# A hybrid attention layer on one core: the mixer's heads as slots in a hand-written TensorE order, the indexer's scores by token tile

## The chip, the cores and the metric

The kernel runs on one core of one Trainium2 chip. The metric is the device time of one execution in microseconds (us), as the median of several runs. TensorE (PE) does matmuls and transposes, VectorE (DVE), ScalarE (ACT) and GpSimd (POOL) work on elements, and SyncE (SP) issues most DMAs.

## What is computed

One decoder layer over 512 tokens with a model width of 1024: a half-step gated feed-forward, a mixer of two groups of heads side by side, a second half-step feed-forward. The mixer is the part that matters here.

```
n  = mod2(PreNorm2(h1));  P = n @ W_in      # q, k, v of group A and B, and q_idx (8 x 64), k_idx (64), w_idx (8)
# group A, 8 heads of 64: sparse attention
ki = rmsnorm(k_idx, g_kidx)
score[t,s] = sum_h w_idx[t,h] * relu(q_idx[t,h] . ki[s]),  -inf where s > t
idx = top_k(score, 128)                     # per token, shared by the heads
attnA = softmax(q.k * D**-0.5 + bias[t5_bucket(t - idx)]) @ v     # over idx alone
# group B, 8 heads of 64: stick-breaking, strictly causal
z = q.k * D**-0.5
between = lax.cumsum(u, axis=3, reverse=True) - u     # u = log_sigmoid(-z) where s < t
attnB = exp(log_sigmoid(z) + between) @ v
o  = [RMSNorm_A(attnA) ; RMSNorm_B(attnB)] @ W_out
```

## The kernel before

**Precision.** Matmuls run on a pair: an operand rounded by ACT (`wh`, line 132) and the rest of it, subtracted on DVE or POOL (`wl`, line 138, the method `split`). A product of 512 columns is three matmuls (`mm3`, lines 276 to 278).

**Stages.** The modulation and the first feed-forward fill the span up to about 404 us, the mixer the span from there to about 735 us, the second feed-forward the rest. The change lies in the mixer alone.

**The indexer.** `proj_block` computes the indexer's keys, its weights and three of its four blocks of queries in four PSUM banks, one half of the tokens after the other. When a bank is complete, its end runs: `end_ki` squares the keys on ACT, takes the rstd on POOL, scales the keys into `k2` (line 716, eight DVE instructions), transposes `k2` on PE (line 719), multiplies by the gain (line 721) and splits the result; `end_q` splits a block of queries and three DMAs on the SP queue lay its halves out for the two heads (`stack`, line 784). Then come the scores: for head after head, of each the token tiles 1, 2 and 3 (256, 384 and 512 keys), two matmuls (793 and 794), a relu on ACT (740) and a weighted sum on DVE (741). Each ends with a `fill`, one step of the next unit's projections.

**Top-k.** `topk` finds the 128 highest scores of a token by 16 rounds of MAX8 (line 772) and MATCH_REPLACE (775) on DVE, and at the end marks the others (`ns`, 778). The rounds of the three tiles are interleaved and handed out after the four units of group B; where they come in DVE's queue is up to the scheduler.

**Units.** A unit is two heads: four of group B, then four of group A. Its projections are 12 steps of six matmuls (four for k, four for q, four for v), plus the loads of their weights. Steps are handed out by `fill` while the unit before works. `end_k` and `end_q` split and stack, `end_q` with its low part on POOL; `end_v` copies by ACT (829), transposes on PE (832) and splits. In `unit`, a head's four score tiles go through `attn_b` (mask matmul 900, two sigmoids 902 and 903, scan 904, product 906) or `attn_a` (mask 919, a DVE reduction 921, exponential 923). `transposed` turns the result in three groups (line 888) and splits them into `pt`, then come the product with v (863), ACT's copy `ot` (868), its transposes (871), and the sum of its two halves (874, 875).

**Order.** No order is written by hand: the scheduler sets one static order for each engine from the program's order, the data and the free buffers. Score tiles live in PSUM banks called `at`, of which there are three; transposes go to `tp`.

Of the kernel before, what the change touches and what calls it, by code (L numbers as in the profile page):

```python
# [23 lines left out]
NT = S // 128  # L24
# [40 lines left out]
class Block:  # L65
# [222 lines left out]
    def proj_block(self, ws, n, banks, ends=()):  # L288

        late = self.turned  # L290
        for half in range(2):
            c = slice(half * 256, half * 256 + 256)
            for b, ((w, m), ps) in enumerate(zip(ws, banks)):
                terms = [(w[0], n[0]), (w[0], n[1]), (w[1], n[0])] if half == 0 else \
# [269 lines left out]
    def o_norm(self, grp, o, oT, tp, pool, bufs=4):  # L564
# [14 lines left out]
        for i in range(NT):  # L579
# [5 lines left out]
            self.normed = self.split(oT[0][:, :, ts], oT[1][:, :, ts], x, nc.vector if i % 2 else nc.gpsimd)  # L585

# [4 lines left out]
    def mixer_out(self, oa, oTb, begun):  # L591
        tc, tp = self.tc, self.tp
        with tc.tile_pool(name="mw", bufs=8, reuse_waits="tile") as mw, \
                tc.tile_pool(name="mo", bufs=4, reuse_waits="tile") as pool:
            oT = [[pool.tile([128, 4, S], F32R, tag=f"oT{c}", name="oT", bufs=1) for c in range(2)], oTb]
            self.o_norm(0, oa, oT[0], tp, pool)
# [8 lines left out]
    def mixer(self, n, po, oT):  # L605
# [3 lines left out]
        with tc.tile_pool(name="mu", bufs=1, reuse_waits="tile") as self.upool, \  # L609
# [3 lines left out]
            steps, ready = zip(*[self.qkv_steps(*c) for c in cols])  # L613
            self.steps = steps[0]
            notsel, top, load = self.indexer()
            o = po.tile([128, NT, 512], F32, tag="oab", name="ob")
            with tc.issue_after(load.ins):
                for n_, (_, _, _, u) in enumerate(cols):
                    if n_ + 1 < len(cols):
                        self.steps = steps[n_ + 1]  # L620
                    else:
                        self.steps, banks = self.out_steps(oT)
                    ou = o[:, :, u * 128:(u + 1) * 128]
                    if n_ < 4:
                        self.unit(ready[n_], self.attn_b, ou)
                        continue
                    if n_ == 4:
                        for step in top:
                            step()
                        U = self.bias_windows()  # L630
                        self.o_norm(1, o, oT, tp, pool, 3)
                        o = po.tile([128, NT, 512], F32, tag="oab", name="oa")
                    den = self.small.tile([128, 4, 2], F32, tag="den", name="den", bufs=2)
                    rd = self.small.tile([128, 4, 2], F32, tag="rd", name="rd", bufs=2)
                    ou = o[:, :, u * 128:(u + 1) * 128]
# [5 lines left out]

    def out_steps(self, oT):

        banks = [self.bank(p) for p in (self.pj, self.pj, self.pj, self.at)]
        cks = []

        def load(n):
# [30 lines left out]
    def indexer(self):  # L678
# [74 lines left out]
        for f in todo + scores(6) + scores(7):  # L753
            f()
            self.fill()
# [204 lines left out]
```

## Time and profile before

| what | value |
|---|---|
| median of three runs | 1100.08 us (1098.58 to 1100.43) |
| the profiled execution's own time | 1099.78 us |
| its span in the trace | 1098.0 us |
| PE busy | 1056.6 us, 96% |
| DVE busy | 583.5 us, 53% |
| ACT busy | 405.6 us, 37% |
| POOL busy | 146.0 us, 13% |

The profile is one execution as the hardware profiler saw it. The span is the time from its first instruction to its last. An engine is busy while an instruction runs on it; a wait is the idle time ahead of an instruction, with what ended it. "PEclk" is the TensorE clock that was granted, as a share of full speed.

### The profile page before, as it was taken

The numbers are of one execution on the slowest core, as the hardware profiler recorded it, in microseconds if no ns is written. First come the engines' busy times: TensorE is split into PE (matmuls) and PEld (weight loads), VectorE is DVE, ScalarE is ACT, GpSimd is POOL, SyncE is SP. The second block draws the span as 40 slices with busy tenths as digits, with TensorE's granted clock in tenths as the row PEclk, the third lists the DMA queues.
The fourth block names the chain that finished last, engine by engine and source line by source line (L and its number), as shares of the span: only waits on it lengthen the run. The fifth ranks groups of instructions, "written<-read, shape, count | busy, mean of one in ns | idle before, by whom it ended". The sixth has DMA issues, their size and how long they took to land.

```text
span 1098.0 us, 13367 instructions
## 1 busy us (share of the span) xinstructions
PE 1056.6 (96%) x5111; PEld 869.1 (79%) x5111; DVE 583.5 (53%) x988; ACT 405.6 (37%) x711; POOL 146.0 (13%) x103
## 2 busy tenths in 40 slices
PE   3899999999999998999999999999999999999997
PEld 2778888888888888877777878789888888888886
DVE  5979888834223174499995444582333333322313
ACT  3342222222212363455556656472232222221221
POOL 2000000000000522423332413320000000000030
PEclk9899999999999999999999999999999999999999
DMA  9969887732222503533334433303333333222222
GB/s 282 294 210 325 297 283 266 248 96 95 91 89 92 164 20 93 144 96 96 92 97 142 132 101 110 116 21 114 96 96 96 96 96 96 96 96 96 96 77 77
DMA packets 171364, 146.06 MB, mean 133 GB/s; under 512 B 7132, under 2 KB 142460, under 8 KB 171300
## 3 DMA queue, kind: packets, MB, share of 16 engines
q1 hardware_dynamic: 169792, 142.97, 42.4%
q10 hardware_dynamic: 1508, 2.24, 0.6%
q8 instruction: 40, 0.66, 0.2%
q14 instruction: 24, 0.20, 0.1%
HBM read 132.04 MB, written 2.13 MB: 122 GB/s over the span
## 4 chain that ended last, share of the span: by engine, by line
PE 82%; DVE 8%; issue 3%; DMA 3%; POOL 2%; ACT 1%; SPq 1%; DVEq 0%; POOLq 0%; ACTq 0%
PE mm L276 15%; PE mm L277 15%; PE mm L278 15%; PE mm L319 8%; PE mm L320 8%; PE mm L318 8%; PE mm L298 3%; PE mm L468 2%; DVE at L904 1%; DMA ra<-in_w_ada_dram 1%; PE at L793 1%; PE at L794 1%; PE tp L888 1%; DMA kq<-kq 1%; POOL rstd L143 1%
## 5 line engine op out<-in xcount | busy, mean ns | idle before, releaser
L132 ACT ACTIVATE wh<-raw 128x1024 fp32r<-128x1024 f32 x156 | 164.3, 1058 | 432.0 <-PE mm L277 139.4
L276 PE MATMUL mm<-nl,wh 128*128 128x512 f32 x808 | 321.2, 398 | 0.0
L277 PE MATMUL mm<-nh,wh 128*128 128x512 f32 x808 | 316.3, 392 | 0.0
L278 PE MATMUL mm<-nh,wl 128*128 128x512 f32 x808 | 316.1, 391 | 0.0
L138 DVE TENSOR_TENSOR wl<-raw,wh 128x1024 fp32r<-128x1024 f32 (+1 forms) x120 | 147.0, 1227 | 223.7 <-ACT wh L132 223.5
L278 PEld LDWEIGHTS mm<-nh,wl 128*128 128x128 f32 x808 | 151.8, 188 | 31.4
L276 PEld LDWEIGHTS mm<-nl,wh 128*128 128x128 f32 x808 | 152.3, 188 | 28.8 <-ACT wh L132 0.3
L277 PEld LDWEIGHTS mm<-nh,wh 128*128 128x128 f32 x808 | 152.0, 188 | 29.0
L320 PE MATMUL mm<-wh,hT 128*128 128x512 f32 x352 | 138.9, 394 | 0.0
L319 PE MATMUL mm<-wh,hT 128*128 128x512 f32 x352 | 138.8, 394 | 0.0
L318 PE MATMUL mm<-wl,hT 128*128 128x512 f32 x288 | 113.9, 396 | 0.0
L138 POOL TENSOR_TENSOR wh<-raw,wh 128x1024 fp32r<-128x1024 f32 x10 | 25.2, 2534 | 653.7 <-ACT wh L132 653.6
L521 DVE TENSOR_TENSOR sg<-sg,mm 128x512 f32<-128x512 f32 x44 | 30.1, 685 | 105.1 <-PE mm L278 91.0
L138 POOL TENSOR_TENSOR wl<-raw,wh 128x1024 fp32r<-128x1024 f32 x27 | 64.7, 2397 | 106.3 <-ACT wh L132 98.1
L320 PEld LDWEIGHTS mm<-wh,hT 128*128 128x128 f32 x352 | 66.2, 188 | 15.6
L319 PEld LDWEIGHTS mm<-wh,hT 128*128 128x128 f32 x352 | 66.2, 188 | 15.5
L153 DVE SCALAR_TENSOR_TENSOR acc<-ra,sc,acc 128x1024 f32<-128x1024 f32 x49 | 62.7, 1279 | 4.5 <-DMA ra<-in_w_ada_dram 4.0
L318 PEld LDWEIGHTS mm<-wl,hT 128*128 128x128 f32 x288 | 54.1, 188 | 13.1
L468 PE MATMUL mm<-nh,wh 128*128 128x512 f32 x96 | 33.7, 429 | 7.2 <-ACT nh L447 6.9
L132 ACT ACTIVATE hT<-sg 128x512 fp32r<-128x512 f32 x44 | 27.8, 632 | 27.4 <-DVE sg L521 27.4
L138 DVE TENSOR_TENSOR pt<-tp,pt 128x512 fp32r<-128x512 f32 (+1 forms) x48 | 27.2, 594 | 18.8 <-ACT pt L132 18.7
L793 PE MATMUL at<-kq 128*128 128x256 f32 (+2 forms) x88 | 31.3, 357 | 3.4 <-DMA kq<-kq 3.4
(208 smaller groups left out, 1244.9 us busy)
## 6 DMA issues: line engine op xcount, KB each, us to landing
ra<-in_w_ada_dram SPq DMA_DIRECT2D x56, 512.0 KB, 5.6
raw<-in_w_ffn_gate_dram SPq DMA_DIRECT2D x44, 512.0 KB, 4.2
raw<-in_w_ffn_up_dram SPq DMA_DIRECT2D x44, 512.0 KB, 4.3
raw<-in_w_ffn_down_dram SPq DMA_DIRECT2D x44, 512.0 KB, 3.4
raw<-in_w_in_dram SPq DMA_DIRECT2D x28, 512.0 KB, 3.5
kq<-kq SPq DMA_DIRECT2D x84, 128.0 KB, 2.4
ra<-in_w_ada_dram SPq DMA_DIRECT2D x32, 256.0 KB, 5.5
raw<-in_w_out_dram SPq DMA_DIRECT2D x8, 512.0 KB, 3.8
```

What stands on the lines that cost most here:

```text
L132: return self.nc.scalar.activation(hi, src, AF.Copy)
L138: return a, (eng or self.nc.vector).tensor_sub(lo, src, hi.bitcast(F32))
L153: nc.vector.scalar_tensor_tensor(acc, raw, sc[:, k:k + 1], acc, op0=ALU.mult, op1=ALU.add)
L276: nc.tensor.matmul(ps[0:m, c], w[0][:, k, :], n[1][:, k, c], start=k == 0, stop=False)
L277: nc.tensor.matmul(ps[0:m, c], w[0][:, k, :], n[0][:, k, c], start=False, stop=False)
L278: return nc.tensor.matmul(ps[0:m, c], w[1][:, k, :], n[0][:, k, c], start=False, stop=k == KD - 1)
L298: mm = self.nc.tensor.matmul(ps[0:m, c], wt[:, k, :], nt[:, k, c], start=j + k == 0, stop=j == 2 and k == KD - 1)
L318: nc.tensor.matmul(ps, lh[:, t], wl, start=n == 0, stop=False)
L319: nc.tensor.matmul(ps, ll[:, t], wh, start=False, stop=False)
L320: nc.tensor.matmul(ps, lh[:, t], wh, start=False, stop=n == len(ks) - 1)
L468: nc.tensor.matmul(banks[j], ws[j][l][:, k, :], n[r][:, k, :], start=k + o == 0, stop=k == KD - 1 and o == 2)
L793: nc.tensor.matmul(ps, q[hd][:, t], kl[hd][:, 0:n], start=True, stop=False)
```

## The change

`unit` falls apart into `product`, `output` and `transposed(h, g)`, and a new function `slot` writes one PE order for the whole mixer after the indexer. A slot handles two heads: of the new head the four score tiles, of the one before it the transposes, the product and the output.

```
+    def slot(self, new, old):
+        for i in range(NT):
+            if new:
+                new["tile"][i]()
+            self.fill()
+            if old and i < 3:
+                self.transposed(old, i)
+        if old:
+            self.fill()
+            self.product(old)
+            self.fill()
+            self.output(old)
+        else:
+            self.fill(2)
```

The mixer calls it under `manual_schedule`, which makes PE's order the program's; the other engines keep the order that the scheduler finds.

```
-            with tc.issue_after(load.ins):
+            with tc.issue_after(load.ins), tc.manual_schedule(engines={mybir.EngineType.PE}):
...
+                for u in range(len(cols)):
+                    self.steps = steps[u + 1]
+                    if u == 4:
+                        for f in top:
+                            f()
+                        U = self.bias_windows(scr)
...
+                        if u == 4 and hd == 1:
+                            for k, f in enumerate(self.o_norm(1, self.o, oT, tp, pool, 3)):
+                                self.steps[2 + k] = both(f, self.steps[2 + k])
...
+            gap = [lambda: None]
+            steps.append([outs[0]] + gap * 2 + [outs[1]] + gap * 2 + [outs[2]] + gap * 2 + [outs[3]] + gap * 2 + outs[4:])
```

So the steps of the last unit are the first products with `w_out`, with empty steps between them, and the norm of group B's output (`o_norm(1)`) is spread over four steps of one slot. The indexer's keys are scaled in two DVE instructions, and their transposes become a call of their own (`end_ki2`), which `proj_block` makes just ahead of the second half of its last bank.

```
-            for i in range(NT):
-                for c in range(2):
-                    nc.vector.tensor_scalar(k2[:, i, c, :], kk[:, i, :], r[:, i:i + 1], None, op0=ALU.mult)
+            nc.vector.tensor_mul(k2[:, :, 0, :], kk, r.unsqueeze(2).to_broadcast([128, NT, 64]))
+            nc.vector.tensor_copy(k2[:, :, 1, :], k2[:, :, 0, :])
...
-        todo = [f for hd in range(6) for f in scores(hd)]
+        todo = [score(*c) for c in [(1, hd) for hd in range(6)] + [(2, hd) for hd in range(3)]
+                + [(1, 6), (1, 7)] + [(2, hd) for hd in range(3, 8)] + [(3, hd) for hd in range(8)]]
...
+        for k, f in enumerate(todo):
+            f()
+            self.fill()
+            if k > 6:
+                tops[0].pop(0)()
+                tops[0].pop(0)()
+        return notsel, tops[0] + [f for fs in zip(*tops[1:]) for f in fs], load
```

The scores go by token tile, tile 1 first and tile 3 last, and 26 of the 33 top-k operations of tile 1 are handed out among the last 13 scores. Two subtractions of the indexer's weights move from POOL to DVE, and the rows of the bias are made earlier (`bias_rows`).

On PE around the indexer's keys (`k` is `k2`, `at` is the fourth bank), before:

```order
L298 MATMUL mm<-nh,wl 128x256 x8
L298 MATMUL mm<-nl,wh 128x256 x8
L298 MATMUL mm<-nh,wh 128x256 x3
L719 MATMUL tp<-ident,k_3174 128x128
L298 MATMUL mm<-nh,wh 128x256 x2
L719 MATMUL tp<-ident,k_3174 128x128
L298 MATMUL mm<-nh,wh 128x256 x2
L719 MATMUL tp<-ident,k_3174 128x128
L298 MATMUL mm<-nh,wh 128x256
L719 MATMUL tp<-ident,k_3174 128x128
L298 MATMUL mm<-nh,wl 128x256 x8
```

and now (line 300 was 298, line 744 was 719, lines 823 and 824 were 793 and 794):

```order
L300 MATMUL mm<-nh,wh 128x256 x8
L300 MATMUL mm<-nh,wl 128x256 x8
L300 MATMUL mm<-nl,wh 128x256 x8
L744 MATMUL tp<-ident,k_3174 128x128 x4
L300 MATMUL at<-nh,wh_3033 128x256 x8
L300 MATMUL at<-nh,wh_3034 128x256 x8
L300 MATMUL at<-nl,wh_3033 128x256 x8
L276 MATMUL mm<-nl,wh 128x512
L277 MATMUL mm<-nh,wh 128x512
L278 MATMUL mm<-nh,wl 128x512
```

The four transposes of the keys stand 21 matmuls later, in one piece.

The first unit's steps run out at the thirteenth of the twenty scores that are handed out after the fourth block of queries, so the last seven, all of 512 keys, stand on PE without a step of a projection between them.

On PE at the end of a unit's projections in group A (line 862 was 832, line 921 was 871), before:

```order
L919 LDWEIGHTS negi
L919 MATMUL at<-ns,negi 128x256
L276 MATMUL mm<-nl,wh 128x512
L832 MATMUL tp<-ident,vt 128x128 x4
L871 MATMUL tp<-ident,ot 128x128 x4
```

and now:

```order
L276 MATMUL mm<-nl,wh 128x512
L277 MATMUL mm<-nh,wh 128x512
L278 MATMUL mm<-nh,wl 128x512
L862 MATMUL tp<-ident,vt 128x128 x4
L921 MATMUL tp<-ident,ot 128x128 x4
L823 MATMUL at<-kq 128x256
```

The transposes of v now stand right behind the last matmul of v, and nothing lies between them but ACT's copy.

On DVE, the last instructions of the top-k (772, 775, and 778 with `ns`) and the work around them, before:

```order
L772 MAX m_4808<-tk 128x8
L775 MATCH_REPLACE tk<-m_4804,tk 128x256
L775 MATCH_REPLACE tk<-m_4806,tk 128x384
L138 TENSOR_TENSOR pt<-tp,pt 128x512 x2
L775 MATCH_REPLACE tk<-m_4808,tk 128x512
L138 TENSOR_TENSOR pt<-tp,pt 128x256
L778 TENSOR_TENSOR ns<-tk,sco 128x256
L778 TENSOR_TENSOR ns<-tk,sco 128x384
L778 TENSOR_TENSOR ns<-tk,sco 128x512
L875 TENSOR_TENSOR ob<-ob,tp 128x4x64
```

and now, around the scan (958) and the product behind it (960) of the sixth head of group B:

```order
L805 MATCH_REPLACE tk<-m_4786,tk 128x512
L958 SCALAR_TENSOR_TENSOR at<-at,ones 128x384
L138 TENSOR_TENSOR pt<-tp,pt 128x256
L960 TENSOR_TENSOR x<-at,x 128x383
L958 SCALAR_TENSOR_TENSOR at<-at,ones 128x512
L808 TENSOR_TENSOR ns<-tk,sco 128x384
L960 TENSOR_TENSOR x<-at,x 128x511
L808 TENSOR_TENSOR ns<-tk,sco 128x512
L138 TENSOR_TENSOR v<-tp,v 128x8x64
L925 TENSOR_TENSOR ob<-ob,tp 128x4x64
```

Before, the three `ns` stood behind the last scan and product of the eighth head; now the top-k ends with those of the sixth, and tile 1's `ns` stands in the first head's slot.

## Rows read from the trace of the kernel before

**Rows 1.** The page: the span, and busy time by engine.
```profile
span 1098.0 us, 13367 instructions
PE 1056.6 (96%) x5111; PEld 869.1 (79%) x5111; DVE 583.5 (53%) x988; ACT 405.6 (37%) x711; POOL 146.0 (13%) x103
```

**Rows 2.** Waits of PE in the mixer: who waited for whom, total, times, longest.
```profile
PE at L793 <- DMA kq<-kq: 3.4, 4, 1.2
PE tp L719 <- DVE k L716: 2.9, 2, 1.9
PE tp L888 <- DVE x L906: 2.3, 5, 0.6
```

**Rows 3.** Busy time in one stretch: length, PE, PEld, DVE, ACT, POOL, PEclk, DMA.
```profile
480.00:500.00 20.00, 18.52 (x101) 14.72 (x99) 19.77 (x51) 9.24 (x20) 7.09 (x4) 1.00 0.40 111
```

**Rows 4.** All engines around one unit's q and the next scores.
```profile
516.01 0.59 ACT L823 ACTIVATE q<-mm 128x512 f32<-128x512 f32 x1
518.19 1.46 PE L863 MATMUL at<-pt,v 128*128 128x512 f32 x8
519.49 0.44 PE L276 MATMUL mm<-nl,wh 128*128 128x512 f32 x1
522.07 0.39 PE L278 MATMUL mm<-nh,wl 128*128 128x512 f32 x1
523.20 0.35 PE L793 MATMUL at<-kq 128*128 128x256 f32 x1 [0.73 <-DMA kq<-kq]
```

**Rows 5.** The granted clock (the number after POOL) behind the second wait for the keys.
```profile
430.00:432.00 2.00, 2.00 (x12) 2.00 (x11) 1.30 (x3) 1.11 (x2) 0.00 (x0) 0.52 0.83 242
```

**Rows 6.** PE's instructions around the indexer's keys: start, length, what, idle before.
```profile
428.82 0.33 PE L719 MATMUL tp<-ident,k 128*128 128x128 f32 x1 [1.90 <-DVE k L716]
429.55 1.61 PE L298 MATMUL mm<-nh,wl 128*128 128x256 f32 x8
434.91 1.07 PE L298 MATMUL at<-nl,wh 128*128 128x256 f32 x8
```

**Rows 7.** Line 716, the eight scalings of the keys: shortest, median, longest in ns.
```profile
L716 DVE TENSOR_SCALAR k<-kk,rstd x8: 242/243/2387, 425.9 to 429.2; 128x64 f32<-128x64 f32 x8
```

**Rows 8.** POOL's instructions at the same time.
```profile
426.20 2.35 POOL L138 TENSOR_TENSOR wl<-raw,wh 128x1024 fp32r<-128x1024 f32 x1 [0.36 <-ACT wh L132]
```

**Rows 9.** The SP queue behind the keys: the DMAs of the pairs.
```profile
431.76 6.63 SPq L784 DMA_DIRECT2D kq<-kq  x8
```

**Rows 10.** The page: the pairs' DMAs: count, KB each, median us from issue to landing.
```profile
kq<-kq SPq DMA_DIRECT2D x84, 128.0 KB, 2.4
```

**Rows 11.** DVE in the mixer by shape: the weighted sum of 512 keys.
```profile
L741 DVE SCALAR_TENSOR_TENSOR sco<-at,wix,sco 128x512 f32<-128x512 f32 x7 | 5.2, 747 | 4.5 <-ACT at L740 4.4
```

**Rows 12.** DVE at the end of the top-k: start, length, what.
```profile
569.63 0.41 DVE L775 MATCH_REPLACE8 tk<-m,tk 128x256 f32<-128x256 f32 x1
569.96 0.08 DVE L775 MATCH_VALUE_LOAD tk<-m,tk 128x8 f32 x1
```

**Rows 13.** DVE from 440 to 580 us by line: busy, mean ns, idle before.
```profile
L904 DVE TENSOR_TENSOR_SCAN at<-at,ones 128x128 f32<-128x128 f32 (+3 forms) x32 | 25.7, 817 | 0.2
L775 DVE MATCH_REPLACE8 tk<-m,tk 128x256 f32<-128x256 f32 (+2 forms) x45 | 24.1, 542 | 0.0
L772 DVE MAX8 m<-tk 128x8 f32<-128x256 f32 (+2 forms) x45 | 23.3, 546 | 0.0
L906 DVE TENSOR_TENSOR x<-at,x 128x127 f32<-128x127 f32 (+3 forms) x32 | 14.8, 476 | 0.0
L138 DVE TENSOR_TENSOR pt<-tp,pt 128x512 fp32r<-128x512 f32 (+1 forms) x24 | 13.5, 590 | 0.2
L778 DVE TENSOR_TENSOR ns<-tk,sco 128x256 bf16<-128x256 f32 (+2 forms) x3 | 4.3, 1478 | 0.0
```

**Rows 14.** All engines around one unit's v: start, length, what, idle before.
```profile
493.53 0.39 PE L278 MATMUL mm<-nh,wl 128*128 128x512 f32 x1
493.95 0.60 ACT L829 ACTIVATE vt<-mm 128x512 f32<-128x512 f32 x1 [3.63 <-PE mm L278]
```

More of the change, by code (lines that the diff above doesn't have):

```diff
@@ L286, in proj, with proj_block @@
         return ps
[L288 removed]
+    def proj_block(self, ws, n, banks, ends=(), mids={}):
         late = self.turned
@@ L585, in o_norm @@
             self.normed = self.split(oT[0][:, :, ts], oT[1][:, :, ts], x, nc.vector if i % 2 else nc.gpsimd)
+        return [lambda i=i: one(i) for i in range(NT)]
     def bank(self, pool):
@@ L612, in mixer @@
             cols = [(C_QB, C_KB, C_VB, u) for u in range(4)] + [(C_QA, C_KA, C_VA, u) for u in range(4)]
-            steps, ready = zip(*[self.qkv_steps(*c) for c in cols])
-            self.steps = steps[0]
-            notsel, top, load = self.indexer()
-            o = po.tile([128, NT, 512], F32, tag="oab", name="ob")
-            with tc.issue_after(load.ins):
[L618 to L635, printed above, removed]
-                    self.unit(ready[n_], lambda hd, qk: self.attn_a(hd, qk, U[u * 2 + hd], notsel, den), ou)
-                    nc.vector.reciprocal(rd, den)
-                    ou = ou.rearrange("p i (h n) -> p i h n", h=2)
-                    nc.vector.tensor_mul(ou, ou, rd.unsqueeze(3).to_broadcast([128, 4, 2, 64]))
@@ L640, in mixer @@
-        return o, banks
+            first, steps, ready = map(list, zip(*[self.qkv_steps(*c) for c in cols]))
+            both = lambda *fs: lambda: [f() for f in fs]
+            loads, outs, banks = self.out_steps(oT)
+            for u in range(len(cols) - 1):
+                steps[u][8] = both(first[u + 1], steps[u][8])
+            for k, f in zip((4, 8), loads):
+                steps[-1][k] = both(f, steps[-1][k])
+            gap = [lambda: None]
+            steps.append([outs[0]] + gap * 2 + [outs[1]] + gap * 2 + [outs[2]] + gap * 2 + [outs[3]] + gap * 2 + outs[4:])
@@ L642, in out_steps @@
+        return self.o, banks
     def out_steps(self, oT):
-        banks = [self.bank(p) for p in (self.pj, self.pj, self.pj, self.at)]
-        cks = []
+        banks, cks = [], []
         def load(n):
@@ L892, in attn_b, with product @@
-    def attn_b(self, hd, qk):
+    def slot(self, new, old):
[10 more added lines that the diff above has]
+            self.output(old)
+        else:
+            self.fill(2)
+    def product(self, h):
+        nc, pool, at = self.nc, self.pool, self.at
+        v, hd = h["v"]["v"], h["hd"]
+        ps = at.tile([128, 512], F32, tag="at", name="at")
+        c = 0
+        for j in range(NT):
+            w = (NT - j) * 128
+            for p in h["pt"]:
+                nc.tensor.matmul(ps[:, j * 128:512], v[:, j, hd, :], p[:, PT_OFF[j]:PT_OFF[j] + w],
+                                 start=c == 0, stop=c == 7)
+                c += 1
+        h["ot"] = pool.tile([128, 512], F32, tag="w2", name="ot", bufs=3)
+        nc.scalar.activation(h["ot"], ps, AF.Copy)
```

142 lines of the change are left out of this document (79 added, 63 removed).

## The prediction

> **What bounds the kernel now.** I read the page first: PE is busy 1056.6 of 1098.0 us [rows 1]. The reader is to see that only some 41 us of the span have no matmul, and that the change, which adds and removes no matmul, can win only from PE's waits and from time at the lower clock. The order of the two programs outside the mixer is the same, so I read the waits of PE in the mixer alone [rows 2]. Three kinds matter: four waits for the DMAs that stack q or k (3.4 us), two for the indexer's scaled keys (2.9), five of a head's transposes for DVE's product (2.3). The last kind comes from a stage in which DVE is full: 19.77 of 20 us while PE has 18.52 [rows 3], and its scans, products and top-k instructions there wait for hardly anything [rows 13]. In that stage it is DVE's work, and where it stands, that sets what PE can do.
>
> **What the change takes away.** A wait costs more than its idle time: the matmul before it lasts 0.39 us, and without a wait the next would start 0.23 us after its start (eleven starts in 2.58 us, from 519.49 to 522.07) [rows 4]. So I add 0.16 us to each.
>
> The waits for DMA: from ACT's copy of q to the first scores with it 7.2 us pass, with PE waiting 0.73 at the end [rows 4]. In the new order the last matmul of q is the second step of a slot. Behind it come four steps of six matmuls (1.39 us each by the pitch of 0.23), a product of 1.3 (518.19 to 519.49 [rows 4]), five groups of transposes (some 1.4) and two score tiles (some 1.1): 9.4 us. That is over the 7.2 by more than the longest of these waits, 1.2 [rows 2]. All four go: 3.4 + 4 x 0.16 = 4.0 us.
>
> The five waits of transposes for DVE go as such, 2.3 + 5 x 0.16 = 3.1 us, and what DVE asks for instead is counted below.
>
> The keys: the two waits are 2.9 us and 0.3 for their ends. Behind them PE ran at 0.52 of its clock, the lower of its two levels (1.2 of 2.4 GHz), for much of 430 to 432 us [rows 5], after an idle of 1.90 [rows 6] and shortly before the other 1.0 of the 2.9 [rows 2]. The 32 matmuls from 429.55 to 434.91 took 5.36 us, where eight at the full clock take 1.07 less 0.16, so 32 take 3.6 [rows 6]; the clock cost 1.7. In all 4.9 us are lost here. What stays: the new transposes stand 21 matmuls later, at about 427.6 us by a pitch of 0.115. Of the eight scalings one took 2.387 us and the median 0.243 [rows 7]; the long one lies over a POOL subtraction from 426.20 to 428.55 [rows 8], and the second wait ended just behind that. The new form has two instructions on DVE from 425.9 on, of about 0.4 each (256 elements took 0.41 [rows 12]), so the second again meets POOL's start at 426.2. If it is blocked, the keys are ready at 428.9, and PE waits 1.3 us. Then the scores: from the last transpose to the DMAs of the pair [rows 9], which start 431.76 in the trace, some 2.4 us pass, and the landing takes 2.4 as the median of the pairs' DMAs [rows 10]; the new order has 24 + 6 matmuls there, 4.2 us, so 0.7 more is waited. I take both, 2.3 with their ends, and a full clock: the gain is 4.9 - 2.3 = 2.6 us, with 4.4 at the upper end and 1.0 at the lower (with the lower clock again).
>
> The Trainium skill, SBUF — State Buffer, "Who interferes with whom", says that a DVE instruction in a mode with two ports, such as a copy or a scaling of 32-bit data, and a GpSimd instruction hold the shared ports in turn, and that the later one is blocked for the whole of the other. It speaks against this edit: the number of DVE instructions is cut, but not the wait behind POOL. Rows 7 agree. By it the sum stands at 2.6; if the new pair slipped past, at 4.4.
>
> Together: 4.0 + 3.1 + 2.6 = 9.7 us.
>
> **What the change costs.** *The end of the indexer.* The last seven score tiles, of 512 keys each, stand together. On PE one is two matmuls of 0.23, 0.46. On DVE it is a sum of 0.747 [rows 11], of which some 0.08 overlaps with the next (a 0.41 long instruction whose follower starts 0.33 on [rows 12]), and between them DVE's order has one of tile 1's top-k instructions, some 0.35: 1.03 a tile. The relu adds some 0.6 ahead of the first (512 columns took ACT 0.60 [rows 14]), and v's low part 0.6 of DVE. PE has three banks, so the fifth of the eleven tiles from there needs the bank of the second, and so on; the first head's first tile comes at about 6.3 us from the start of the seven, where PE's own work is 3.6. I take 2.7 us, between 1 (if DVE's top-k work slipped behind) and 5 (with the lower clock).
>
> *The heads of group B.* DVE's work in the first six slots, from rows 13 with 0.08 off for each instruction: scan and product of a head (25.7 + 14.8 - 5.1) / 8 = 4.4, six heads 26.5. Top-k: 24.1 + 23.3 less 7.2 is 40.2 for 15 rounds of three tiles, with the first round and the value loads 46.3, of which tile 1 has about a quarter, and 26 of its 32 operations are done before: 37.2 remain. The marks 4.3. The low parts of `pt` 1.45 a head, five heads 7.2. Low parts of v and k and the sums of the outputs, 5. Together 80 us. PE's work in the same slots: six steps 8.3, score tiles 1.8, transposes 1.1, product 1.3, output 0.4, and v's transposes 0.4 in every second: 13.3 or 12.9, and 10.4 in the first: 76 us. Before, the same work had eight heads' time; now, by the order, the last mark stands in the sixth slot, and slots seven and eight leave DVE half empty. So PE waits for 4 us at least. Going along the order by hand, it waits in four places for together 10 (the second, third and fifth slot's transposes, and v's transposes of the sixth, since ACT's queue holds a DMA for a buffer of the top-k ahead of v's copy). I take 7 us, nearer to the sum, range 3 to 11.
>
> *Transposes of v.* In every slot that ends a unit's projections they stand right behind v's last matmul. ACT's copy starts 0.42 us after that matmul's start and lasts 0.60 [rows 14], so PE goes on at 1.03 where it could at 0.23: 0.8 us. In the first units DVE's wait covers it; in the four last it is paid, 3.2 us.
>
> *Rest.* The norm of group B's output stands in one slot with its chain ACT, DVE, POOL ahead of its transposes: 0.5, between 0 and 2. In the last unit the step ahead of `output` is empty, so that `ot` waits for its copy as v does, in two slots: 1.6.
>
> Together: 2.7 + 7.0 + 3.2 + 0.5 + 1.6 = 15.0 us. Against 9.7 that is 5.3 slower: the profiled execution would go from 1099.8 to 1105.1 us. It stands 0.3 below the median of 1100.08, so the forecast is 1105.4.
>
> **The rivals.** *DVE keeps up (faster).* If the heads' work on DVE trails by less than PE's banks and buffers allow, the first two costs fall to 1 and 1, the keys slip past POOL (4.4) and the rest stays: 11.5 - 7.3 = 4.2 faster, 1095.9; with half of v's waits covered too, 1094. For it speaks that PE in the present order waits only 2.3 us for a DVE that is just as full [rows 2, 3]; against it that the same work now has six slots. It decides where PE's waits in the six slots sum to under 2 us. *The gains and costs cancel.* With 3 for the heads and 1 for the indexer's end, costs and gains are 9.3 and 9.7: 1099.7. *The clock drops (slower still).* If the indexer's end or two of the slots idle as the keys do now, each drop costs what it did there, 1.7 [rows 6, 5], and the heads cost 10: 1105.4 + 3 + 3.4 = 1112. The wait is then one of two or more of over 1 us close together; a lone idle of 0.88 in 480 to 500 left that stretch at 1.00 [rows 3].
>
> The Trainium skill, TensorE: Matmul & The Clock Gate, "HAM oscillation — how this bites in real kernels", says that short bursts of matmuls between waits are throttled again and again. By that rule every slot with two waits would pay as the keys did, six slots 10 us, 1115; rows 5 bear it out at one place only, and rows 3 speak against it for single waits. I give it 3 in 100.
>
> **How the numbers follow.** The forecast with its near bounds (over 1102.3) has 0.40, the drop of the clock in one or two places 0.09, in every slot 0.03: slower by over 0.2% (about what a measurement of this kernel can tell from no change) 0.52. Cancelling has 0.14. DVE keeping up has 0.34. The range from 1093 to 1111 leaves out the throttled slots and the far ends, about 1 or 2 in 10; cases of both signs hold most of the chance, and the forecast's own range is 1102 to 1110.
>
> **What would show it.** Right: no wait for DMA on the stacked pairs in group B; a wait of about 1 us at line 744 behind POOL; waits at lines 823 and 942 between the indexer's end and the sixth slot that sum to near 10; waits of 0.8 at line 862 in group A. DVE full from the indexer's end to the sixth slot and half empty behind it. Wrong, if PE's busy share in the six slots stays as it is: then DVE trails without harm, and the time falls. Wrong too if line 744 has no wait, or if the granted clock is below 1.00 in the heads.

## The result, and the profile after

The changed kernel takes 1115.24 us (median, 1113.62 to 1117.01) where the one before took 1099.89 beside it: 1.0142 times as long, with a 95% interval from 1.0124 to 1.0160. The forecast was 1105.4, in a range up to 1111. The sign came as forecast, the size was a third of what came, and the time lies above the range. The profiled execution took 1115.25 us with a span of 1113.4, so 15.4 us were added to the 1098.0 of [rows 1].

The waits of PE in the mixer, changed kernel (who waited for whom: total, times, longest), stand against [rows 2]:

```profile
PE tp L862 <- ACT vt L859: 7.4, 7, 1.6
PE at L823 <- DMA kq<-kq: 4.6, 2, 2.7
PE tp L202 <- DVE pt L138: 3.3, 2, 2.0
PE at L823 <- DVE sco L767: 2.1, 4, 1.1
...
PE tp L921 <- ACT ot L911: 1.5, 2, 0.7
...
PE tp L942 <- DVE pt L138: 0.8, 3, 0.3
PE tp L942 <- DVE v L138: 0.6, 1, 0.6
```

The reader is to see that of the three kinds of [rows 2] two are gone (the keys, line 719 before and 744 now, and the heads' products, 888 and 942), and that five others have come (a sixth, of 0.2 us, is not listed). All waits of the mixer sum to 23.6 us in 28 places, where the kernel before had 12.2 in 19. With 0.16 us for the end of the matmul ahead of each, as in the prediction, that is 12.8 us more.

The rest is the clock. The stretches behind two of the waits (length, PE, PEld, DVE, ACT, POOL, PEclk, DMA), changed kernel:

```profile
470.00:472.00 2.00, 2.00 (x8) 1.61 (x7) 1.18 (x5) 0.10 (x1) 0.00 (x0) 0.51 0.22 59
472.00:474.00 2.00, 2.00 (x7) 1.52 (x7) 1.41 (x5) 0.56 (x2) 0.00 (x0) 0.63 0.00 0
610.00:612.00 2.00, 2.00 (x6) 1.58 (x5) 1.11 (x2) 0.84 (x2) 0.74 (x1) 0.50 0.03 8
612.00:614.00 2.00, 2.00 (x11) 1.80 (x11) 0.00 (x0) 0.01 (x1) 0.54 (x1) 0.65 0.00 0
```

PE ran at the lower of its levels for much of the next 4 us each time, as it had behind the keys in [rows 5]: two drops where there was one. PE was busy all through these stretches, so what the clock lacks to 1.00 in each, times its 2 us, is time lost: 0.98 + 0.74 = 1.7 us behind the first wait and 1.7 behind the second, the price of the prediction. One drop more and 12.8 us of waits are together 14.5 of the 15.4 us.

The shares by term, each with 0.16 for every wait, forecast and measured in the two profiles (two kinds of 0.3 and 0.2 us, one gone and one new, are left out):

| term | forecast | measured |
|---|---|---|
| the keys, with their lower clock | -2.6 | -4.9 |
| waits for the pairs' DMAs | -4.0 | +0.9 |
| the heads' transposes for DVE | -3.1 + 7.0 | -2.3 |
| the indexer's end, DVE's sums | +2.7 | +2.7 |
| transposes of v | +3.2 | +8.5 |
| the norm of group B | +0.5 | +3.6 |
| the last unit's outputs | +1.6 | +1.8 |
| splits of `pt` in group A | 0 | +0.9 |
| the clock, behind the indexer's end and the norm | 0 | +3.4 |
| sum | +5.3 | +14.6 |

Where the largest new waits come from can be read in the same trace. **The pairs.** The SP queue's DMAs of the second unit's q, and the score that waits for them:

```profile
489.89 8.98 SPq L814 DMA_DIRECT2D kq<-kq  x3
```
```profile
498.40 0.46 SPq L814 DMA_DIRECT2D kq<-kq  x1
```
```profile
kq<-kq SPq DMA_DIRECT2D x1, 128.0 KB, 8.4
```
```profile
499.06 0.36 PE L823 MATMUL at<-kq 128*128 128x256 f32 x1 [2.71 <-DMA kq<-kq]
```

The first line spans the issues of all three and not a landing; the second is the issue of the third DMA alone. That DMA overwrites what the first one reads, and is issued only at 498.40. The third line, from the list of DMA issues (count, size, us from issue to landing), shows why: the first DMA, issued at 489.89, landed 8.4 us later, where [rows 10] has 2.4 as the median of one and where the same DMA of the kernel before took 3.9. At 489.14 to 491.3 four loads of the bias windows (256 KB each) were issued from ACT's queue. The other wait of the 4.6, 1.90 us at 468.80, is the first unit's; ACT's rows show why:

```profile
453.79 0.58 ACT L853 ACTIVATE q<-mm 128x512 f32<-128x512 f32 x1
...
460.03 0.61 ACT L859 ACTIVATE vt<-mm 128x512 f32<-128x512 f32 x1 [0.81 <-PE mm L278]
460.54 0.64 ACT L132 ACTIVATE kq<-q 128x512 fp32r<-128x512 f32 x1
```

The copy of q was ready at 454.4, and its rounding came at 460.5, where the kernel before had 0.3 us between them. The rounding waits for a buffer: there are 13 of the kind `kq`, and scores by token tile keep the four blocks of indexer queries alive until the tiles of 512 keys. That is read from the program; the run with scores in pairs tests it.

**v.** Four of the seven waits are for ACT's copy alone (0.69 to 0.75 us). In the other three ACT had something else ahead; here a rounding of weights, in ACT's order ahead of the copy:

```profile
643.11 1.06 ACT L132 ACTIVATE wh<-raw 128x1024 fp32r<-128x1024 f32 x1 [0.66 <-PE mm L277]
644.08 0.58 ACT L859 ACTIVATE vt<-mm 128x512 f32<-128x512 f32 x1
```
```profile
644.71 0.66 PE L862 MATMUL tp<-ident,vt 128*128 128x128 f32 x4 [1.46 <-ACT vt L859]
```

**The norm.** DVE's scalings of line 584, POOL's rows beside them, and the transposes behind:

```profile
602.07 1.29 DVE L584 TENSOR_SCALAR ob<-ob,rstd 128x512 f32<-128x512 f32 x1
...
604.48 3.52 DVE L584 TENSOR_SCALAR ob<-ob,rstd 128x512 f32<-128x512 f32 x2
```
```profile
603.92 2.38 POOL L138 TENSOR_TENSOR wl<-raw,wh 128x1024 fp32r<-128x1024 f32 x1 [0.84 <-ACT wh L132]
606.26 1.45 POOL L138 TENSOR_TENSOR oT<-no,oT 128x512 fp32r<-128x512 f32 x1
```
```profile
609.09 0.63 PE L202 MATMUL tp<-ident,ob 128*128 128x128 f32 x4 [2.04 <-DVE pt L138]
```

The two scalings that fell beside POOL's subtractions took 3.52 us; the first of the four took 0.48. In DVE's order the reduction of a score tile and the split of `pt` stand behind them, so PE waits for the split, though the scalings are what is late.

### The profile page after: what moved, and what is told of

Its sections match the earlier page's. It is cut to its first block, busy times and chain, and to the rows that moved or that the text cites. A ratio compares the mean times of both kernels' runs of the same rounds, so it can differ in the third digit from the quotient of the medians.

```text
span 1113.4 us, 13353 instructions
## 1 busy us (share of the span) xinstructions
PE 1061.4 (95%) x5104; PEld 871.0 (78%) x5111; DVE 588.1 (53%) x984; ACT 408.9 (37%) x711; POOL 141.9 (13%) x101
## 5 line engine op out<-in xcount | busy, mean ns | idle before, releaser
L138 DVE TENSOR_TENSOR wl<-raw,wh 128x1024 fp32r<-128x1024 f32 (+1 forms) x122 | 149.5, 1227 | 241.4 <-ACT wh L132 241.2
L138 POOL TENSOR_TENSOR wl<-raw,wh 128x1024 fp32r<-128x1024 f32 x25 | 60.2, 2410 | 105.1 <-ACT wh L132 98.5
L823 PE MATMUL at<-kq 128*128 128x256 f32 (+2 forms) x88 | 34.6, 394 | 6.8 <-DMA kq<-kq 4.6
```

What stands on the lines that cost most here:

```text
L138: return a, (eng or self.nc.vector).tensor_sub(lo, src, hi.bitcast(F32))
L823: nc.tensor.matmul(ps, q[hd][:, t], kl[hd][:, 0:n], start=True, stop=False)
```

## The experiments

Two theories stood against each other. **Queues (Q):** PE's fixed order meets single late steps, and what is late stands in ACT's, POOL's or the DMAs' queues. **DVE (D):** the prediction's own main cost, DVE's load in the first six slots. The ratios below are to the kernel before, in runs on the same chip; the changed kernel's own is 1.0142.

The clock differs between these runs too, and it has to be kept apart from the waits. In the profiles of scores by head and of later bias windows PE ran at the full clock all through the mixer, so 3.4 us of their gain on the changed kernel's profile are clock; in those of the norm on ACT and of half of the top-k it ran at the lower level for longer than in the changed kernel's. The sections say what that hides.

### The keys' part alone

```diff
-                    nc.vector.tensor_scalar(k2[:, i, c, :], kk[:, i, :], r[:, i:i + 1], None, op0=ALU.mult)
+            nc.vector.tensor_mul(k2[:, :, 0, :], kk, r.unsqueeze(2).to_broadcast([128, NT, 64]))
+            nc.vector.tensor_copy(k2[:, :, 1, :], k2[:, :, 0, :])
...
+                        {3: end_ki2})
```

> The kernel before with the keys' part of the change alone: two DVE instructions for the scaling, and the four transposes 21 matmuls later. In the trace of the change the wait for the keys and the lower clock behind it are gone. If that is due to this part, the time is 4 to 5 us under the kernel before (about 1095.4). If the second DVE instruction is blocked by POOL as the prediction had it, and the change's trace shows no wait only because other work was late there, the gain is 2.6 or less and a wait of about 1 us stands at the transposes.

Measured: 1096.72 us, 0.9952 (0.9935 to 0.9968), so 5.3 us less. In its waits the keys don't stand any more, and the others are those of before, somewhat longer for the DMAs:

```profile
PE at L799 <- DMA kq<-kq: 3.8, 4, 1.3
PE tp L894 <- DVE x L912: 2.3, 5, 0.6
```

This part wins more than the 4.4 us that the prediction had as its upper end, and it is the fastest kernel of the study. Not all of the 5.3 is the keys: the waits and the drop that went are 4.9 us in the profile, and the mean granted clock of the five runs is 0.997 against 0.994 of the kernel before beside them, by estimate some 3 us, where the drop at the keys is 1.7.

### Scores by head again

```diff
-        todo = [score(*c) for c in [(1, hd) for hd in range(6)] + [(2, hd) for hd in range(3)]
...
+        todo = [score(i, hd) for hd in range(8) for i in range(1, NT)]
...
-                tops[0].pop(0)()
```

> The changed kernel with the indexer's scores by head again and no top-k operation among them; slots, keys and all else stay. Theory Q (PE's fixed order is held up at single places, by what stands in ACT's, POOL's and the DMAs' queues): the waits at the indexer's end, 2.1 us for DVE's sums and 1.9 for the pair of the first q, go with the clock's drop behind them, 6 us in all: about 1109. Theory D (DVE has the work of eight heads in six slots): with the 26 early top-k operations moved into the slots, DVE has some 9 us more to do there and PE waits longer: 1115 or more.

Measured: 1108.40 us, 1.0066 (1.0041 to 1.0091), 0.75% less than the changed kernel. Of the waits at the indexer's end 0.8 us are left, and the pair's wait is 0.5. Waits for DVE at v's low part grew from 0.6 to 2.3, which is D's direction, but not its size:

```profile
PE tp L938 <- DVE v L138: 2.3, 2, 1.2
...
PE at L819 <- DVE sco L767: 0.8, 2, 0.6
PE at L819 <- DMA kq<-kq: 0.5, 1, 0.5
```

Of the 8.3 us, 3.4 are the two drops of the clock, which this profile doesn't have. The one behind the norm is gone although the norm's waits, 1.30 and 2.04 us, are those of the changed kernel.

### Scores in pairs of heads

```diff
+        todo = [score(*c) for c in [(1, hd) for hd in range(6)] + [(2, 0), (2, 1), (3, 0), (3, 1)]
+                + [(1, 6), (1, 7)] + [(i, hd) for h in (2, 4, 6) for i in (2, 3) for hd in (h, h + 1)]]
...
```

> The changed kernel with the scores of the tiles 2 and 3 taken in pairs of heads, so that a block of indexer queries is done with early and its buffers come free; tile 1 stays first and its top-k early. Theory Q with buffers as the cause: the rounding of the first unit's q, which stood behind the fourth score tile of 512 keys on ACT, comes some 5 us earlier, the wait of 1.9 us for its pair goes and the seven tiles in a row are broken up: 4 to 6 us less, 1109 to 1111. If the wait is due to the place of q's rounding behind v's copy for another reason, it stays: 1115.

Measured: 1115.33 us, 1.0124 (1.0101 to 1.0147). The mechanism is as expected; ACT's rows:

```profile
455.52 0.58 ACT L853 ACTIVATE q<-mm 128x512 f32<-128x512 f32 x1
...
456.41 0.62 ACT L132 ACTIVATE kq<-q 128x512 fp32r<-128x512 f32 x1
```

The rounding comes with the copy and the first unit's wait for its pair is gone, so the buffers were the cause of this wait. The gain is not there: the second unit's pair then waited 2.94 us, DVE's split of v 3.2 us in two places, and behind both the stretches of 6 us from 494 and from 556 us ran at a granted clock of 0.72. What was saved ahead was waited for later.

### v's transposes later

```diff
+            st["vt"] = vt
+
+        def end_v2():
+            vt = st["vt"]
...
+                steps[u + 1][0] = both(steps[u + 1][0], ready[u]["end_v2"])
```

> The changed kernel with the transposes of v behind the first step of the next slot instead of right behind v's last matmul. Theory Q: seven waits of 0.7 to 1.6 us, 7.4 in all, with 0.16 each for the matmul's end go: 8.5 us less, about 1107. Theory D: the waits at the transposes of v only take up time that PE would wait for DVE anyway in the first units; then three go to waits for DVE, and the gain is 4 to 5: 1110.

Measured: 1110.07 us, 1.0074 (1.0052 to 1.0095), 0.67% less. Six of the seven waits are gone, one of 0.2 is left; the pair of the second unit waited longer:

```profile
PE at L825 <- DMA kq<-kq: 4.3, 1, 4.3
...
PE tp L949 <- DVE ob L932: 2.1, 2, 1.5
```

The waits for v had covered part of the wait for the pair, and part of DVE's.

### The bias windows later

```diff
...
+            self.tc.add_manual_dep(ld.ins, self.ots[-2].ins.name, NOSYNC, reason="issue order")
```

> The changed kernel with all eight loads of the bias windows issued from ACT's queue behind the output copy of the seventh slot, where four of them stood in the second slot and four in the sixth ahead of v's copy. If these loads (1 MB in the second slot) delay the pairs' DMAs, the wait of 2.7 us for the second unit's pair goes, and the wait of 1.6 at the sixth slot's transposes of v falls to 0.7: 3.7 to 4.5 us less, 1111. If DVE's work in the six slots is the bound, this time comes back as waits for DVE: 1114 or 1115.

Measured: 1112.30 us, 1.0090 (1.0074 to 1.0107), 0.51% less. The SP queue's row for the second unit's q:

```profile
489.51 4.30 SPq L816 DMA_DIRECT2D kq<-kq  x3
```

The row is 4.30 us instead of 8.98 (the first DMA lands after 3.8 instead of 8.4), and there is no wait for it; v's wait of 1.6 in the sixth slot is 0.69. At DVE 0.7 us more is waited. So the early loads were the cause of this wait, and DVE took back little. The waits alone explain about half of the 5.7 us; this profile, the fastest of its four, has none of the changed kernel's two drops of the clock.

### The norm's scalings on ACT, and later in the slot

```diff
-            nc.vector.tensor_scalar(o[:, i, :], o[:, i, :], r[:, i:i + 1], None, op0=ALU.mult)
+            nc.scalar.activation(o[:, i, :], o[:, i, :], AF.Copy, scale=r[:, i:i + 1])
```

> The changed kernel with the four scalings of group B's norm on ACT instead of DVE. In the trace of the change they took 0.48, 1.29 and together 3.52 us on DVE, the long ones while POOL made a low part, and PE waited 1.28 and 2.04 us behind them, with the clock at 0.50 and 0.65 of full speed afterwards. If POOL's hold on DVE is the cause: the second wait and the lower clock go, 3.5 to 4 us less, 1111.5; the first stays, since the norm's chain is not done. If the chain itself is too late for its slot: both waits stay, 1115.

Measured: 1117.38 us, 1.0142 (1.0124 to 1.0160): no gain. The two waits of 3.3 us became one of 2.4, for the chain itself:

```profile
PE tp L202 <- ACT ob L584: 2.4, 1, 2.4
```

All waits of the mixer, with their ends, are 1.8 us less than in the changed kernel. The clock hides it: from 460 us on, stretches of 20 us were granted 0.83, 1.00 and 0.91 where the changed kernel had 0.91, 1.00 and 1.00, and 0.91 from 600 on in both. The mean of the four runs is 0.990, that of the changed kernel's four 0.9925.

Then the same with the first three of the four groups one step later:

```diff
-                                self.steps[2 + k] = both(f, self.steps[2 + k])
+                                self.steps[(3, 4, 5, 5)[k]] = both(f, self.steps[(3, 4, 5, 5)[k]])
```

> The changed kernel with the norm's scalings on ACT and its four groups of transposes one to two steps later in the slot (the steps 3, 4, 5, 5 instead of 2, 3, 4, 5). With the scalings on ACT alone one wait of 2.4 us was left, at step 2, for a chain of squares, POOL's rstd and the scaling that is not done by then. If the place in the slot is the rest of the cause, that wait goes and the time falls by the 3.3 us of the two waits and by the lower clock where it follows them: 3.5 to 5 us, 1110 to 1112. If the chain delays something else in the slot (the exponentials of the new head stand behind the scalings on ACT), the gain is under 2.

Measured: 1116.84 us, 1.0144 (1.0122 to 1.0166): again no gain. Of the norm's waits 0.6 us are left, but ACT's queue, which now has the scalings too, made the next transposes of v wait 2.35 instead of 0.75:

```profile
618.23 0.66 PE L862 MATMUL tp<-ident,vt 128*128 128x128 f32 x4 [2.35 <-ACT vt L859]
```

All waits together are 2.5 us less than in the changed kernel, and the time still didn't fall. The profiled execution, the slowest of its four, was granted 0.74 from 460 to 480 us and 0.83 from 500 to 520, against 0.91 and 1.00 in the changed kernel; the mean of the four runs is 0.989. By itself this run settles nothing on the size of the norm's part.

### Half of the top-k

```diff
-            if k > 6:
+            if 6 < k < 15:
...
-        return [top, drop] * (TOPK // 8)
+        return [top, drop] * (TOPK // 16)
...
```

> The changed kernel with half of the top-k: 8 rounds a tile instead of 16, so that the attention of group A sees the 64 highest scores less than it should. It leaves some 20 us of DVE's work out of the first six slots and 1 to 2 out of the indexer's end. Theory D (DVE's load there sets the time): the waits of PE for v, the pair and the sums between 460 and 560 us shrink by 5 or more: 1108 to 1110. Theory Q: of these waits, 2.1 us at the score tiles fall to 1 or so, the pairs' and v's stay as they are: 1113.5 to 1115.

Measured: 1115.95 us, 1.0128 (1.0109 to 1.0147), so 0.14% less, inside the interval of no difference. The stretches of its heads, with DVE's busy time as the third of the busy times, against the 20.00 that DVE was busy from 520 to 540 us in the changed kernel:

```profile
500.00:520.00 20.00, 18.60 (x89) 15.28 (x90) 12.22 (x26) 8.13 (x19) 2.72 (x2) 0.83 0.45 122
520.00:540.00 20.00, 19.31 (x105) 15.41 (x104) 12.35 (x21) 11.81 (x27) 7.09 (x4) 1.00 0.38 106
```

DVE is busy for 12 of 20 us, and PE waits as long for v and the pairs as in the changed kernel: 6.5 + 5.3 us against 7.4 + 4.6. So these waits don't come from DVE's load, and D falls as their explanation. The 0.14% is not the price of that load, though. All waits with their ends are 2.5 us less here, and the profiled execution, the slowest of its four at 1118.61, lost some 4.7 us more to the clock than the changed kernel's, by the same sum as above over stretches of 1 us and PE's busy time in them (it was granted 0.74 from 460 to 480 us and 0.83 from 500 to 520); the mean of the four runs is 0.990. Why the clock was lower no run shows. Under "What DVE's load is worth" the same halving is held against a kernel without a drop on either side.

### Together

The changed kernel with scores in pairs of heads, v's transposes and the bias windows later, the norm's scalings on ACT without their new place, the whole top-k, and besides:

```diff
-            self.fill()
+            if k == 0 or k > 7:
+                self.fill()
...
+                for _ in range(min(3, len(self.top)) if new["u"] < 4 else 0):
+                    t = self.top.pop(0)()
+                    if t is not None:
+                        self.tc.add_manual_dep(t.ins, self.last.ins.name, NOSYNC, reason="issue order")
```

> The changed kernel with all of it together: scores in pairs of heads with the steps of the projections moved to the last of them, the transposes of v behind the next slot's first step, the bias windows behind the seventh slot, the norm's scalings on ACT, and what is left of the top-k handed out three operations behind each score tile of group B, kept there in DVE's order. If DVE had too much in the first six slots, the even hand-out takes that away, and nothing but the norm's first wait, the last unit's two and the tail's is left: 1100 - 5 for the keys - 4 for the pairs - 3 for DVE's products, and 2 to 3 back: 1090 to 1092. If the manual order costs in itself, it stays over the 1095.4 of the keys alone.

Measured: 1106.22 us, 1.0037 (1.0022 to 1.0052). It missed the expected 1090 to 1092 by 14 us. It made waits of its own, 2.8 us of the bias rows' matmul for a bank that DVE's split of k held, and 2.4 for two pairs, and it kept the norm's 2.4:

```profile
PE mm L684 <- DVE kq L138: 2.8, 1, 2.8
PE tp L202 <- ACT ob L584: 2.4, 1, 2.4
PE at L827 <- DMA kq<-kq: 2.4, 2, 1.3
```

So the parts were joined again one by one, on scores by head. First scores by head and v later:

> The changed kernel with two parts mended: the indexer's scores by head, and the transposes of v behind the next slot's first step. Alone the first gave 0.8% and the second 0.7%, and the second was partly given back at the second unit's pair, which waited 4.3 us behind the early loads of the bias windows; by head these loads come after the top-k. Theory Q: the two add up, and no such wait comes: 1.5% to 1.7% under the changed kernel, which is 0.1% under to 0.2% over the kernel before. Theory D: waits for DVE in the heads take their place, and the gain is 1% or less.

Measured: 1102.83 us, 1.0016 (1.0006 to 1.0025): 1.24% less than the changed kernel, where the two alone gave 0.75% and 0.67%. They nearly add up, and no wait for a pair is left. This profile, and those of the next three runs, have no drop of the clock in the mixer, so they can be held against each other by their waits. What DVE takes back is now seen:

```profile
PE tp L202 <- DVE pt L138: 3.3, 2, 2.0
PE tp L945 <- DVE ob L928: 3.0, 3, 1.6
```

With the norm on ACT and later:

> As the kernel with two parts mended, and the norm on ACT and later as well. If the norm's slot gives 3.5 to 5 us by itself, this is 0.2% to 0.5% faster than the kernel before, which is about what the keys' part gives alone: then the slots cost and win nothing once their local waits are gone.

Measured: 1099.17 us, 0.9984 (0.9971 to 0.9997). The norm's part gives 0.32%, 3.5 us, here, where v's transposes don't stand behind ACT's queue: its waits fall from 3.3 to 0.6 and 0.4. With the last unit's products moved:

```diff
-            steps.append([outs[0]] + gap * 2 + [outs[1]] + gap * 2 + [outs[2]] + gap * 2 + [outs[3]] + gap * 2 + outs[4:])
+            steps.append([outs[0]] + gap * 4 + [outs[1], outs[2]] + gap * 4 + [outs[3]] + outs[4:])
```

> As the one with three parts mended, and in the last unit the products with the output's weights stand right ahead of the head's output instead of ahead of its second score tile, so that the copy of the output is covered: two waits of 0.75 and their ends, 1.8 us, go; against it the three groups of transposes there have less between them, and two waits of 0.26 for their splits may grow to 0.6 each. So 0 to 1.8 us under the kernel with three parts: 0.3% to 0.6% faster than before.

Measured: 1098.86 us, 0.9979 (0.9969 to 0.9988). The waits at the outputs fell from 1.5 to 0.4 us, the one at the norm of group A grew by 0.4, and the time by no more than the interval allows. The version that beats both kernels most is still the unit order with the keys' part, 0.9952.

### What DVE's load is worth

> The slots with three parts mended (scores by head, v's transposes later, the norm on ACT and later) and half of the top-k, 8 rounds a tile instead of 16, so that group A's attention sees the 64 highest scores less. In the mended slots 5.4 us of waits for DVE were left before the eighth head, at the score sums, the products, v's low part and the output's sums. If they are DVE's load, 3 to 4 us go: 0.4% to 0.5% under the mended slots, to about 0.994 of the kernel before. If they are chains of single steps, the time stays within 1 us.

Measured: 1098.33 us, 0.9971 (0.9959 to 0.9983), 0.13% less than with the whole top-k, where 0.4% to 0.5% were expected for a load of DVE and under 1 us for chains of single steps: it lies between, at 1.4 us, and far from the 7 us of the prediction. The waits for DVE at the transposes fell from 3.8 us to 1.6, and the ones for ACT's copies (`ot`, and the split of `pt`) grew from 1.7 to 3.0:

```profile
PE tp L945 <- DVE v L138: 0.7, 2, 0.4
...
PE tp L945 <- DVE ob L928: 0.6, 1, 0.6
```

> The kernel before with the keys' part, and half of the top-k in the same way. Its waits for DVE at the transposes are 2.8 us, and the ones for the pairs' DMAs 3.8. If DVE's load is behind the first only: 2.5 to 3 us less than with the keys alone, 0.993. If PE's order, which the scheduler writes anew, moves the DMAs' waits too, more. The two kernels with half of the top-k are then to be held against each other: equal means that the slots' order costs nothing beyond DVE; the slots over 1 us slower means that something else of theirs stays.

Measured: 1098.77 us, 0.9978 (0.9969 to 0.9987): 0.26% more than with the whole top-k, so the expectation was wrong in its sign. The scheduler wrote PE's order anew, and the waits for DVE grew although DVE was busy for only 8.74 of the 20 us from 540 on:

```profile
PE at L799 <- DMA kq<-kq: 4.5, 4, 1.4
PE tp L894 <- DVE x L912: 3.2, 7, 0.6
```

This points to waits for the end of a chain (sigmoid, scan, product) rather than for room on DVE; no run took the chain apart. Held against each other, as the expectation wants, the two kernels with half of the top-k are equal within their intervals, 0.9971 and 0.9978. By its rule the slots' order would then cost nothing beyond DVE; but they are equal because this one grew slower, so it is no proof. Last, v later and the bias windows later in the changed kernel:

> The changed kernel with v's transposes later and the loads of the bias windows later, the scores as changed. Alone they gave 0.7% and 0.5%, the first with 1.6 us given back at the pair that waits behind these loads. If they are independent causes, 1.3% to 1.5% go, to 1.000 or 1.001 of the kernel before. If DVE takes the place of what goes, as it did by 1 to 2 us with each alone, the gain is 0.9% to 1.1%, to 1.004.

Measured: 1105.40 us, 1.0041 (1.0026 to 1.0055): 1.0% less, where the two alone gave 1.2%. Waits for DVE of 4.5 us stand in the heads, so some of the gain went to DVE, as the second expectation had it.

## Why the prediction was wrong

**What held, and what was luck.** The change costs more in the slots than it wins at the keys. But the sign was right by luck: it hung on the 7.0 us for DVE in the heads. With the 0.8 that came in their place the prediction's own sum is 0.9 us faster than before, and what made the kernel slower are terms that it had at less than half their size (v, the norm), at nothing (the clock) or as a gain (the pairs). The indexer's end was sized right for DVE's sums (2.7 forecast, 2.7 measured), the last unit's outputs nearly (1.6, 1.8), and v's transposes do wait for ACT's copy, 0.7 to 0.75 us where nothing else is in its way.

**The step that failed most: DVE in the heads of group B.** The sum of 80 us of DVE's work against 76 of PE's was turned into 7 us of waits. They did not come: the profile has 0.6 there, and half of the top-k leaves the waits for v and the pairs as they are. The sum wasn't false, DVE was busy for 20.00 of 20 us between 520 and 540. But PE was held up already by the pair (2.7), by v (three times) and at the indexer's end, and DVE worked on meanwhile. Where these waits were mended, waits for DVE of 4 to 5 us came up, about what the sum had as its floor; of the 3.8 left with the norm mended too, 2.2 went with half of the top-k, so only a part of them is load. The prediction added a cost that stands beside other waits as if it stood behind them.

**v's transposes.** The term was right in kind and mis-sized: 0.8 us in four places forecast, 1.2 us in seven measured. Two steps were wrong. ACT was taken as free when v's last matmul ends; in its order stood a rounding of weights (1.06 us, 1.46 in all) or a copy behind loads that wait for the top-k (1.58). And the first units' waits were put down as covered by DVE, which had no wait of its own there.

**The pairs.** The step counted PE's time between the last matmul of q and the first score with it, 9.4 us, against the 7.2 of before, and left out what stands between. In the first unit the rounding waits for a buffer that the new order of scores frees late (scores in pairs bring it back to the copy); in the second the first DMA lands after 8.4 us, since the loads of the bias windows were hoisted into the second slot (with the loads issued later it is 3.8, and there is no wait). The prediction had priced only the later four of these loads, for their place in ACT's queue, and the early four not at all.

**The norm.** Its slot was priced at 0.5 us for the chain. The waits are 3.3: 1.3 for the chain, whose first scaling starts only at 600.60 us, and 2.0 behind two scalings that lay beside POOL's subtractions. With the scalings on ACT 2.4 us were still waited, and 0.6 with the groups one step later: the chain's place in the slot is the larger part. The Trainium skill, SBUF — State Buffer, "Who interferes with whom", by which the later of such two instructions is blocked for the whole of the other, was used in the prediction for the keys and not for these four instructions of the same kind. The trace agrees with it here: 3.52 us for two scalings, 0.48 for one that lay free.

**The keys.** The same rule was applied at the keys, with a block of 2.4 us for the second of the new instructions. There the rows of the change don't show it:

```profile
427.42 0.29 DVE L737 COPY k<-k 128x256 f32<-128x256 f32 x1
```
```profile
427.77 2.40 POOL L138 TENSOR_TENSOR wl<-raw,wh 128x1024 fp32r<-128x1024 f32 x1 [0.84 <-ACT wh L132]
```

The copy ended at 427.71, and POOL started 0.06 later. Which came first was a matter of 0.35 us, from one start to the other, and the prediction chose the wrong side. It also had the transposes at 427.6 us, and they came at 428.83, so that a copy done 1 us later would still have been in time. The part alone won 5.3 us and not 2.6.

**The clock.** A drop at the indexer's end or in two slots was the third rival, at 0.09, and it is what the profile shows, twice, 3.4 us. Its time, 1112, was near the result, but that came by way of v, the pairs and the norm and not of DVE's 10 us. The number nearest to the result is 1115, of the rival with a drop in every slot, at 0.03; that is luck, since two drops came and not six. The forecast's own sum had no new drop.

What stays open is the difference of 0.3% between the slots with three parts mended and the keys alone: the waits in the two profiles differ by 1.5 us in 3 places more, 2.0 with their ends, and their spans by 3.2. Some 1.3 of the 3.2 lie ahead of the indexer's keys (DVE's instruction that writes the indexer's weights, `wix`, starts at 424.98 us against 423.71). Nothing was tried on the rest: no run took by itself the two subtractions that moved from POOL to DVE or the earlier rows of the bias.

## What to carry to other kernels

An order that is written for one engine alone fixes that engine's order and leaves the others' to the scheduler, so each step in it should be held against what stands ahead on the engine that feeds it, and against the buffers and DMA loads that the new order frees or hoists. Waits that lie side by side don't add up: a load summed against PE's time should be held against the local waits in the same stretch before it is added to them, since the other engine works on while PE waits; here the sum came up, in about its size, only once those waits were mended. An edit that takes waits away can show no gain in time when the clock drops more often in its runs, so the granted clock is to be read beside the waits. A change of several parts is best made one at a time; here the keys' part won 0.48% and the rest lost four times as much.

## What the runs showed of the hardware

The lower clock doesn't follow the waits alone. At the indexer's end the changed kernel waited 1.90 us at 468.80, after four shorter waits, and then ran at 0.51. The kernel with later bias windows waited 2.23 us at the same place, after the same four, and ran on at the full clock:

```profile
468.00:470.00 2.00, 0.01 (x1) 0.04 (x1) 2.00 (x6) 0.38 (x1) 0.00 (x0) 1.00 0.45 92
470.00:472.00 2.00, 2.00 (x11) 1.70 (x11) 1.01 (x6) 0.45 (x2) 0.00 (x0) 1.00 0.43 107
```

The norm's two waits, 1.3 and 2.0 us, stand unchanged in the profiles of scores by head, later transposes of v and later bias windows, and none of the three has the drop that the changed kernel's has behind them. So behind the same waits a drop came in one profile and not in another, and each is worth some 1.7 us, more than several of the gains looked for here. The Trainium skill, TensorE: Matmul & The Clock Gate, "What you observe", says that under steady matmuls the moment of the change of clock varies by half a microsecond from run to run. These profiles differ by more: whole drops come or stay away.

The first of a pair's three DMAs, 128 KB, landed 8.4 us after its issue when four loads of 256 KB were issued from another queue between 0.75 us ahead of it and 0.61 behind, and after 3.8 us without them.
